# Last RMSNorm of a decoder trunk: second half's squares and factor in PSUM, one activation table for logarithm and exponential, two outputs on GpSimd

## The chip, the cores and the metric

The kernel runs on one NeuronCore of a Trainium2 chip. The metric is the device time of one execution in microseconds (us); the median over runs is compared. The engines are called by their names in the profile: PE is TensorE (PEld its weight loads), DVE is VectorE, ACT is ScalarE, POOL is GpSimd, and SP is SyncE, which here only issues DMAs.

## What is computed

A two-layer decoder trunk on a sequence of 1024 tokens of width 1024, in float32: each layer has a pre-norm mixer (the first a retention and an RWKV-7 group, the second sliding-window attention) and a SwiGLU FFN, both added to the residual `h`. At the end stands one more RMSNorm, which is what the change is about:

```python
def rms_norm(x, g):
    xf = x.astype(jnp.float32)
    y = xf * lax.rsqrt(jnp.mean(xf * xf, axis=-1, keepdims=True) + RMS_EPS)
    return (y * g.astype(jnp.float32)).astype(x.dtype)

def reference(x, ...):
    h = x
    for layer in range(DEPTH):          # DEPTH = 2
        n = rms_norm(h, norm1_g[layer])
        ...
        h = h + mix
        n = rms_norm(h, norm2_g[layer])
        h = h + swiglu(n, ffn_w_gate[layer], ffn_w_up[layer], ffn_w_down[layer])
    return rms_norm(h, final_g)
```

## The kernel before

The residual stands transposed in SBUF: features on the 128 partitions, in 8 tiles (`h(k)`, k = 0 to 7) of 512 tokens, for each of two halves of the sequence (`hf` 0 and 1). Matrix products split each float32 operand into a high and a low part (`split`, `vsplit`, `wsplit`) and do three matmuls for each product: ScalarE casts the high part (lines L356 and L1348), GpSimd or VectorE subtracts to get the low part (L358, L1349), and `prod` issues the three matmuls (L1175 to L1177).

The FFN's down projection (`down`) treats the two halves of the sequence and pairs of output columns together, with sums and differences of blocks (one level of a Strassen-like scheme), so that each product goes into more than one column's sum. Its helper `vop` holds every VectorE addition of it, so all of them have the line L1375: `u<-ps_m,u` and `y<-ps_r,u` gather products, `h<-h,u` and `h<-h,ps_f` add to the residual. In the last group of the last layer the columns of half 0 get their final values first. `down` then hands back control (`yield`), the last norm of half 0 is traced, and the rest of `down` follows: four products into the banks `f`, `f`, `f`, `y`, each of which is added to h(1), h(3), h(5), h(7) of half 1, and then four more on top of them in the same banks, which are added to h(0), h(2), h(4), h(6). The PSUM pool of this phase has three banks `f`, two `m`, and one each of `r`, `c` and `y`. The one bank `c` and the bank `r` last hold products of the phase before these eight.

`final_r` computes one half's factor. For each of the 8 columns, in the order in which they get ready, ScalarE squares `h(k)` into an SBUF tile `nq` (L1626) and multiplies `h(k)` in place by the norm's gain (L1627); VectorE adds the square to the running sum, in place in the square's tile (L1629). A matmul with a constant matrix of 1/1024 (L1632) sums over the partitions and gives every partition the mean: one for the sum of the first seven squares and one for the eighth. A float32 matmul shows as two records. ScalarE then takes the logarithm (L1634) and exp(-0.5 x) (L1635) into the tile `y`. When a function is not in the activation table set that ScalarE holds, a table load stands before it, with the same line. `final_out` multiplies `h(k)` by the factor (L1642) and stores it with a DMA on SP's queue (L1643): 256 KB each, all of half 0 on GpSimd and all of half 1 on VectorE.

The order in which each engine works its queue is settled when the program is built: a scheduler with a timing model takes the traced instructions as they become ready, and prefers those that were traced earlier. So squares of half 0 stand on ScalarE between the weight casts of the last products. `keep` pins an instruction behind the one that was traced before it on the same engine. Each engine works its queue in order.

Of the kernel before, what the change touches and what calls it, by code (L numbers as in the profile page):

```python
# [12 lines left out]
AF = mybir.ActivationFunctionType  # L13
ALU = mybir.AluOpType
AX = mybir.AxisListType

P = 128
T = 1024
HT = 512
# [185 lines left out]
class Kern:  # L205
# [1411 lines left out]
    def final_r(self, hf, pool, order, n):  # L1617


        nc = self.nc  # L1620
        h = self.kt(self.h[hf])
        ps = self.pst("m", [P, HT])
        acc = None
        for i, k in enumerate(order):
            sq = self.t(self.pp, [P, HT], "nq", 4)
            nc.scalar.activation(sq, h(k), AF.Square)  # L1626
            nc.scalar.activation(h(k), h(k), AF.Copy, scale=self.col("nf", k))  # L1627
            if 0 < i < n:
                nc.vector.tensor_tensor(out=sq, in0=acc, in1=sq, op=ALU.add)  # L1629
            acc = sq  # L1630
            if i >= n - 1:
                nc.tensor.matmul(ps, self.cst["ones"], sq, start=i == n - 1, stop=i == KT - 1)  # L1632
        r = self.t(pool, [P, HT], "y", 2)
        nc.scalar.activation(r, ps, AF.Ln, bias=self.cst["eps"][:, 0:1])  # L1634
        nc.scalar.activation(r, r, AF.Exp, scale=-0.5)  # L1635
        return r

    def final_out(self, hf, r, order, engines):
        nc = self.nc
        h = self.kt(self.h[hf])  # L1640
        for k, e in zip(order, engines):
            (nc.gpsimd if e == "p" else nc.vector).tensor_tensor(out=h(k), in0=h(k), in1=r, op=ALU.mult)  # L1642
            nc.sync.dma_start(self.out[k, :, hf * HT : (hf + 1) * HT], h(k))  # L1643


def trunk(tc, A, out):
    with ExitStack() as ctx:
        K = Kern(ctx, tc, A, out)
# [4 lines left out]
        def close(*gs):  # L1653
            for g in gs:
                g.__exit__(None, None, None)

        def run(f):
            for _ in f:
                pass
# [55 lines left out]
        r = K.factor_of(1, sp, "c")  # L1715
# [43 lines left out]
        r = K.factor_of(1, sp)  # L1759
# [17 lines left out]
        f = K.down(1, fp, fz, K.form_down(1, NP - 1, x, ts), X)  # L1777
        next(f)
        order = (0, 2, 4, 6, 1, 3, 5, 7), (1, 3, 5, 7, 0, 2, 4, 6)
        r0 = K.final_r(0, fz, order[0], 7)  # L1780
        run(f)
        r1 = K.final_r(1, fz, order[1], 7)
        K.final_out(0, r0, order[0], "pppppppp")
        K.final_out(1, r1, order[1], "vvvvvvvv")
        close(gp, gf, gz, K.ghx, g1, gy)


# [53 lines left out]
```

## Time and profile before

| | us |
|---|---|
| median of 3 runs | 2376.92 |
| lowest and highest run | 2371.43, 2380.17 |
| profiled execution | 2374.81 |
| its span in the profile | 2373.0 |
| mean granted TensorE clock | 0.99 |
| busy: PE, DVE, ACT, POOL | 2312.1, 1667.4, 1054.7, 948.4 |

The span is what the records of the profile cover; the execution's own time is 1.81 us longer. Busy times are sums of instruction durations. Times of single instructions below count from the span's start, so that 2340 lies 33 us before its end. "DVE nq L1629" is a VectorE instruction of line 1629 that writes a tile `nq`; "issue" in the chain is time in which nothing is waited for.

### The profile page before, as it was taken

What the parts mean: (1) busy time and instruction counts of PE and PEld (TensorE: products, weight loads), DVE (VectorE), ACT (ScalarE), POOL (GpSimd) and SP (SyncE); (2) the same over time, 40 slices, a digit from 0 to 9 for tenths busy, and PEclk for the clock granted to TensorE, in tenths of its full rate; (3) what the DMA queues carried; (4) which work ended last, traced back from release to release, by engine and by line L of the source; (5) the groups of instructions that cost most, each with busy time, mean ns of one, the idle gap of its engine ahead of it and who ended that gap; (6) DMA issues with size and microseconds to landing.
All of it is one profiled execution on the core that took longest, in us unless ns stands there. A gap on an engine that the chain in (4) does not pass through costs nothing. (4 is left out here: it accounts for less than half of the span.)

```text
span 2373.0 us, 35626 instructions
## 1 busy us (share of the span) xinstructions
PE 2312.1 (97%) x13092; PEld 1828.9 (77%) x13092; DVE 1667.4 (70%) x2630; ACT 1054.7 (44%) x1946; POOL 948.4 (40%) x746
## 2 busy tenths in 40 slices
PE   8999999999999999999999999999999999999997
PEld 6777777777777888888778877777787888877885
DVE  6876865774667358887675668567548778888776
ACT  5354533324456333333333556557645333333335
POOL 3123221201342057776667300002103577767665
PEclk9999999999999999999999999999999999999998
DMA  7555544443445545554554321232236465547652
GB/s 271 203 199 197 176 154 132 128 115 114 148 164 183 208 164 206 211 197 163 218 220 142 123 66 64 71 127 71 100 128 221 170 216 213 209 175 280 245 193 87
DMA packets 167741, 395.92 MB, mean 167 GB/s; under 512 B 42896, under 2 KB 45584, under 8 KB 167568
## 3 DMA queue, kind: packets, MB, share of 16 engines
q1 hardware_dynamic: 164448, 388.15, 47.8%
q10 hardware_dynamic: 2832, 4.45, 0.5%
q8 instruction: 104, 1.70, 0.3%
q0 software_dynamic: 288, 1.05, 0.1%
q14 instruction: 69, 0.57, 0.1%
HBM read 271.29 MB, written 116.92 MB: 164 GB/s over the span
## 5 line engine op out<-in xcount | busy, mean ns | idle before, releaser
L240 PE MATMUL ps_f<-n,w 128*128 128x512 f32 x1440 | 385.6, 415 | 8.6 <-ACT w L335 6.4
L240 PEld LDWEIGHTS ps_f<-n,w 128*128 128x128 f32 x1440 | 268.2, 192 | 93.6 <-issue 24.5
L335 ACT CAST w<-wr 128x512 fp32r<-128x512 f32 x244 | 147.9, 612 | 182.9 <-PE ps_f L352 73.1
L336 POOL TENSOR_TENSOR w<-wr,w 128x512 fp32r<-128x512 f32 x68 | 92.1, 1363 | 280.0 <-ACT w L335 223.0
L336 DVE TENSOR_TENSOR w<-wr,w 128x512 fp32r<-128x512 f32 (+1 forms) x176 | 123.8, 706 | 71.5 <-ACT w L335 71.3
L336 POOL TENSOR_TENSOR w<-wq,w 128x512 fp32r<-128x512 f32 x92 | 130.5, 1431 | 29.2 <-ACT w L335 27.2
L351 PE MATMUL ps_f<-n,w 128*128 128x512 f32 x356 | 141.7, 398 | 0.0
L352 PE MATMUL ps_f<-n,w 128*128 128x512 f32 x356 | 141.0, 396 | 0.6 <-POOL w L336 0.6
L350 PE MATMUL ps_f<-n,w 128*128 128x512 f32 x356 | 140.8, 396 | 0.6 <-ACT n L1601 0.5
L1182 DVE TENSOR_TENSOR nq<-ps_m,u 128x512 f32<-128x512 f32 x88 | 58.8, 685 | 104.3 <-PE ps_m L1177 104.2
L336 POOL TENSOR_TENSOR wx<-wr,wx 128x512 fp32r<-128x512 f32 x8 | 10.6, 1319 | 301.8 <-ACT wx L335 301.6
L1175 PE MATMUL ps_f<-n,w 128*128 128x512 f32 x298 | 118.5, 398 | 4.7 <-DVE h L1375 3.1
L1175 PE MATMUL ps_m<-n,w 128*128 128x512 f32 x300 | 117.5, 392 | 1.5 <-DVE h L1375 1.5
L1176 PE MATMUL ps_f<-n,w 128*128 128x512 f32 x298 | 117.2, 393 | 0.1
L1176 PE MATMUL ps_m<-n,w 128*128 128x512 f32 x300 | 116.8, 389 | 0.0
L1177 PE MATMUL ps_m<-n,w 128*128 128x512 f32 x300 | 116.8, 389 | 0.0
L1177 PE MATMUL ps_f<-n,w 128*128 128x512 f32 x298 | 116.7, 393 | 0.0
L358 POOL TENSOR_TENSOR n<-nq,n 128x512 fp32r<-128x512 f32 x54 | 91.5, 1707 | 8.9 <-ACT n L356 8.9
L1175 PE MATMUL ps_m<-cb,w 128*128 128x512 f32 x240 | 93.4, 389 | 1.0 <-DVE nq L1182 1.0
L1176 PE MATMUL ps_m<-cb,w 128*128 128x512 f32 x240 | 93.4, 389 | 0.0
L1177 PE MATMUL ps_m<-cb,w 128*128 128x512 f32 x240 | 93.4, 389 | 0.0
L1349 POOL TENSOR_TENSOR w<-wd,w 128x512 fp32r<-128x512 f32 (+1 forms) x53 | 76.0, 1444 | 34.8 <-ACT w L1348 34.8
(525 smaller groups left out, 6467.1 us busy)
## 6 DMA issues: line engine op xcount, KB each, us to landing
hc<-n SPq DMA_DIRECT2D x74, 512.0 KB, 2.6
wsp<-w SPq DMA_DIRECT2D x54, 512.0 KB, 3.3
w<-wsp SPq DMA_DIRECT2D x54, 512.0 KB, 3.4
wq<-in_w_gate SPq DMA_DIRECT2D x44, 512.0 KB, 4.3
u<-u SPq DMA_DIRECT2D x88, 256.0 KB, 2.9
n<-hc SPq DMA_DIRECT2D x43, 512.0 KB, 5.5
wr<-in_w_in SPq DMA_DIRECT2D x34, 512.0 KB, 4.8
hid<-n SPq DMA_DIRECT2D x66, 256.0 KB, 2.0
```

The lines of the kernel that those rows point to most:

```text
L240: self.nc.tensor.matmul(out, lhsT, rhs, **kw)
L335: nc.scalar.copy(hi[:, :n], raw[:, c])
L336: self.lo.tensor_tensor(out=lo[:, :n], in0=raw[:, c], in1=hi.bitcast(F32)[:, :n], op=ALU.subtract)
L350: nc.tensor.matmul(ps, hi, rh, start=k == 0, stop=False)
L351: nc.tensor.matmul(ps, hi, rl, start=False, stop=False)
L352: nc.tensor.matmul(ps, lo, rh, start=False, stop=k == n - 1)
L358: e.tensor_tensor(out=lo, in0=src, in1=hi.bitcast(F32), op=ALU.subtract)
L1175: mm(ps, hi, xh, start=first and k == 0, stop=False, skip_group_check=True)
L1176: mm(ps, hi, xl, start=False, stop=False, skip_group_check=True)
L1177: mm(ps, lo, xh, start=False, stop=last and k == len(w) - 1, skip_group_check=True)
L1182: add = lambda o, x, y: V.tensor_tensor(out=o, in0=x, in1=y, op=ALU.add)
L1349: nc.gpsimd.tensor_tensor(out=lo, in0=v, in1=hi.bitcast(F32), op=ALU.subtract)
```

## The change

In the second half, the squares that are added (all but the first and the last) are written to the PSUM bank `c`, and the running sum goes to an SBUF tile `nq` of its own. The second half's factor is written twice by two exponentials of the same logarithm: first into the PSUM bank `r`, for VectorE, which makes six outputs with it, and then into SBUF, for GpSimd, which makes the last two. An activation table set that holds logarithm and exponential is loaded ahead of both factors, pinned behind the last ScalarE instruction traced so far (a cast of the last products' inputs). The first half is otherwise as it was, with all its outputs on GpSimd.

```diff
@@ final_r(self, hf, pool, order, n)
         ps = self.pst("m", [P, HT])
         acc = None
         for i, k in enumerate(order):
-            sq = self.t(self.pp, [P, HT], "nq", 4)
+            if hf and 0 < i < n:
+                sq = self.pst("c", [P, HT])
+            else:
+                sq = self.t(self.pp, [P, HT], "nq", 4)
             nc.scalar.activation(sq, h(k), AF.Square)
             nc.scalar.activation(h(k), h(k), AF.Copy, scale=self.col("nf", k))
             if 0 < i < n:
-                nc.vector.tensor_tensor(out=sq, in0=acc, in1=sq, op=ALU.add)
+                o = self.t(self.pp, [P, HT], "nq", 4) if hf else sq
+                nc.vector.tensor_tensor(out=o, in0=acc, in1=sq, op=ALU.add)
+                sq = o
             acc = sq
             if i >= n - 1:
                 nc.tensor.matmul(ps, self.cst["ones"], sq, start=i == n - 1, stop=i == KT - 1)
         r = self.t(pool, [P, HT], "y", 2)
         nc.scalar.activation(r, ps, AF.Ln, bias=self.cst["eps"][:, 0:1])
+        if not hf:
+            nc.scalar.activation(r, r, AF.Exp, scale=-0.5)
+            return r, None
+        rp = self.pst("r", [P, HT])
+        nc.scalar.activation(rp, r, AF.Exp, scale=-0.5)
         nc.scalar.activation(r, r, AF.Exp, scale=-0.5)
-        return r
+        return r, rp
 
     def final_out(self, hf, r, order, engines):
         nc = self.nc
         h = self.kt(self.h[hf])
         for k, e in zip(order, engines):
-            (nc.gpsimd if e == "p" else nc.vector).tensor_tensor(out=h(k), in0=h(k), in1=r, op=ALU.mult)
+            if e == "p":
+                nc.gpsimd.tensor_tensor(out=h(k), in0=h(k), in1=r[0], op=ALU.mult)
+            else:
+                nc.vector.tensor_tensor(out=h(k), in0=h(k), in1=r[1], op=ALU.mult)
             nc.sync.dma_start(self.out[k, :, hf * HT : (hf + 1) * HT], h(k))
@@ trunk
         next(f)
         order = (0, 2, 4, 6, 1, 3, 5, 7), (1, 3, 5, 7, 0, 2, 4, 6)
+        K.keep(tc.nc.scalar.preload_act_table_set("natural_log_exp_and_others"))
         r0 = K.final_r(0, fz, order[0], 7)
         run(f)
         r1 = K.final_r(1, fz, order[1], 7)
         K.final_out(0, r0, order[0], "pppppppp")
-        K.final_out(1, r1, order[1], "vvvvvvvv")
+        K.final_out(1, r1, order[1], "vvvvvvpp")
```

## The prediction

> **What bounds the kernel now.** I read the head of the profile's page first, then the chain of work that ended last, in order of time, for the last 40 us, then the groups of instructions by line for the same stretch, and last the busy time in short windows. Times are microseconds from the span's start.
>
> ```profile
> span 2373.0 us, 35626 instructions
> PE 2312.1 (97%) x13092; PEld 1828.9 (77%) x13092; DVE 1667.4 (70%) x2630; ACT 1054.7 (44%) x1946; POOL 948.4 (40%) x746
> ```
>
> TensorE is busy 97% of the span, so no edit on another engine can move anything but the stretches in which TensorE has run out of work. The timeline has the last matmuls of two of the four column groups of the final GEMM, three groups apart:
>
> ```profile
> 2345.51 0.39 PE L1177 MATMUL ps_f<-n,w 128*128 128x512 f32 x1
> ...
> 2351.63 0.39 PE L1177 MATMUL ps_y<-n,wr 128*128 128x512 f32 x1
> ```
>
> So a group takes (2351.63 - 2345.51) / 3 = 2.04, its results are there at 2345.90, 2347.94, 2349.98 and 2352.02, and then 2373.0 - 2352.0 = 21 us are left in which only the last norm runs. Everything the change touches lies there or shortly before. The chain through it (start, duration, engine, written tile, line):
>
> ```profile
> 2340.98 1.08 DVE nq L1629
> 2342.05 0.61 DVE h L1375
> 2342.69 0.64 ACT nq L1626
> 2343.35 0.72 ACT h L1627
> 2344.09 1.28 ACT L1634
> 2345.39 0.69 ACT y L1634
> 2346.09 1.28 ACT L1635
> ...
> 2348.02 0.53 ACT nq L1626
> 2348.57 1.36 DVE nq L1629
> ...
> 2351.24 1.66 DVE nq L1629
> ...
> 2354.18 1.60 DVE nq L1629
> ...
> 2357.09 1.62 DVE nq L1629
> 2358.74 3.39 PE ps_m L1632 x4
> 2362.16 0.69 ACT y L1634
> 2362.86 1.28 ACT L1635
> 2364.15 0.65 ACTq L1836
> ...
> 2364.82 0.69 DVE h L1642
> ```
>
> The pieces without a tile at L1634 and L1635 are table loads, 1.28 each. Three of them are on the chain; the second half's logarithm has its load beside the matmul. The middle is one loop, four times over: add of a square (L1629), residual add of the next column (L1375), square of it (L1626), add. It runs 2.9 a turn although TensorE delivers a column every 2.04: the columns wait for the loop. Why the adds are slow is in the groups (busy us, mean ns | idle before):
>
> ```profile
> L1642 POOL TENSOR_TENSOR h<-h,y 128x512 f32<-128x512 f32 x8 | 11.7, 1504 | 6.6 <-ACT y L1635 6.6
> L1629 DVE TENSOR_TENSOR nq<-nq,nq 128x512 f32<-128x512 f32 x6 | 8.0, 1333 | 9.0 <-ACT nq L1626 9.0
> ...
> L1642 DVE TENSOR_TENSOR h<-h,y 128x512 f32<-128x512 f32 x8 | 4.9, 686 | 5.5 <-ACT y L1635 5.5
> ...
> L1375 DVE TENSOR_TENSOR h<-h,ps_f 128x512 f32<-128x512 f32 x4 | 2.7, 674 | 0.0
> ```
>
> With both inputs in SBUF and GpSimd busy, a VectorE add takes 1333 on average; with GpSimd idle the same shape takes 686 (L1642); with one input in PSUM 674, though GpSimd was multiplying beside most of them. GpSimd pays too:
>
> ```profile
> 2351.05 1.30 POOL L1642 TENSOR_TENSOR h<-h,y 128x512 f32<-128x512 f32 x1
> 2352.29 1.73 POOL L1642 TENSOR_TENSOR h<-h,y 128x512 f32<-128x512 f32 x1
> ```
>
> 1.30 with no SBUF-only VectorE add beside it, 1.73 with one.
>
> **The change part by part.** The sum is made against the profiled execution: 2374.81, a span of 2373.0 and 1.81 around it. That is 2.1 below the median of the runs shown, 2376.92.
>
> *Squares in PSUM.* Six adds (the second half's) get one PSUM input; I take 0.68 for each, by the L1375 row. The first, 1.08 at 2340.98, has a GpSimd subtraction beside it (L1349, last row of the next fence) and leads to the first half's logarithm: 0.40 less. Then 1.36, 1.66, 1.60 and 1.62 become 0.68: 0.68 + 0.98 + 0.92 + 0.94 = 3.52. (The second of the six does not wait for GpSimd and gains nothing.) No row has ScalarE writing PSUM; the nearest are its reads:
>
> ```profile
> 2297.25 0.59 ACT L1410 COPY u<-ps_f 128x512 f32<-128x512 f32 x1 [1.04 <-PE ps_f L1177]
> ...
> 2334.82 0.68 DVE L1375 TENSOR_TENSOR u<-ps_c,u 128x512 f32<-128x512 f32 x1
> ...
> 2340.49 1.02 POOL L1349 TENSOR_TENSOR wr<-ws,wr 128x384 fp32r<-128x384 f32 x1 [2.09 <-ACT wr L1348]
> ```
>
> From 0.59 to the logarithm's 0.69, so a square, now 0.64, changes by -0.05 to +0.05; over five squares and the exponential on the path that is -0.3 to +0.3. I take 0, since the operation stays the same. [...]
>
> The new wait: the one bank "c" makes the next square wait for the add before it. Behind a square in ScalarE's queue stand the scale copy (L1627) and the logarithm; VectorE's next add waits for all that. It costs nothing: the next square already waits for L1375, which VectorE runs after that add. If that order changed, the cover would go, and the price is the one add, 0.68. The bank's last reader in the GEMM is a VectorE operation that ended by 2335.5 (2334.82 and 0.68), before the first such square.
>
> *One table, loaded ahead.* Loads at 2344.09 and 2346.09 vanish, 2 x 1.28 = 2.56 off the chain, since ScalarE is the last to be ready there (the square at 2348.02 starts behind the exponential). The load at 2362.86 vanishes: 1.28. The new load stands on ScalarE behind the last cast traced before it:
>
> ```profile
> 2318.89 0.62 ACT L356 CAST n<-hr 128x512 fp32r<-128x512 f32 x1
> 2319.71 0.63 ACT L1626 ACTIVATE nq<-h 128x512 f32<-128x512 f32 x1 [0.20 <-DVE h L1375]
> 2320.24 0.50 ACT L1348 CAST w<-wd 128x384 fp32r<-128x384 f32 x1
> ...
> 2321.75 2.89 POOL L1349 TENSOR_TENSOR w<-wd,w 128x384 fp32r<-128x384 f32 x2
> ...
> ACT w L1348 <- PE ps_r L1177: 1.8, 2, 1.5
> ```
>
> It takes 2319.5 to 2320.8, so the square and the weight cast move by about 1.1. Cover: the GpSimd half of that cast's split does not start before 2321.75 in this trace, and casts of this stretch wait up to 1.5 for TensorE to free a buffer (last row). 0, at worst 1.28. [...] The chain has 0.02 between the scale copy's end (2344.07), the load, and the logarithm (2345.39), so I count the load alone.
>
> *What is late next.* Take 0.40 + 2.56 and the add savings off the four residual adds and they want to start at 2346.30, 2348.27, 2350.25 and 2352.22, against TensorE's 2345.90, 2347.94, 2349.98 and 2352.02: the loop only just stays behind the GEMM. TensorE is the floor; at most 0.2 more can come out of this loop.
>
> *The ones-matmuls* (L1632), unchanged in code, change in speed:
>
> ```profile
> 2341.68 1.02 PE L1632 MATMUL ps_m<-nq,c_ones 128*128 128x512 f32 x2
> ...
> 2354.00:2355.00 1.00, 0.00 (x0) 0.00 (x0) 0.81 (x1) 0.87 (x2) 1.00 (x2) 0.88 0.11 43
> 2355.00:2356.00 1.00, 0.00 (x0) 0.00 (x0) 1.00 (x2) 0.00 (x0) 1.00 (x2) 0.50 0.57 219
> ```
>
> A pair took 1.02 for the first half; for the second, after 6.7 of idle TensorE and at a granted clock of 0.50 (the figure after POOL's), two pairs took 3.39. After the change TensorE idles 0.2 before the first pair and 0.5 before the second, so the clock stays. From the last add's end: residual add 0.61, square 0.66, weight load 0.2, pair 1.02, together 2.5 where it was 3.46 (2358.70 to 2362.16): 0.9 less (0 if the clock fell).
>
> *Six outputs on VectorE, two on GpSimd.* The factor is written twice; the copy for GpSimd comes one exponential (0.65) later. VectorE would end after 6 x 0.61 + 0.1 = 3.8 instead of 4.9, GpSimd after 0.65 + 2 x 1.30 = 3.3 if its eight products of half 0 are done: they start about 3.0 earlier, at 2345.1, and at 1.3 each end at 2355.5, before the factor at 2356.1. The two stores stand last on SP, so nothing waits behind them. But the stores are the limit:
>
> ```profile
> 2366.00:2371.60 5.60, 0.00 (x0) 0.00 (x0) 3.73 (x7) 0.00 (x0) 0.00 (x0) 0.50 0.97 374
> ...
> 2367.00:2368.00 1.00, 0.00 (x0) 0.00 (x0) 1.00 (x3) 0.00 (x0) 0.00 (x0) 0.50 1.07 412
> ```
>
> The DMA share is 0.97 over the 5.6 us in which the eight outputs leave, at about 410 GB/s when full: 8 x 256 KB at that rate is 5.1, more than either multiply time. First output to end stays as it is, 8.2 after the exponential. I count 0 (at best 1.1).
>
> *Sum:* 0.40 + 2.56 + 3.52 + 0.9 + 1.28 = 8.7. Span 2364.3, execution 2366.1; from the median, 2376.92 - 8.7 = 2368.2.
>
> **The rivals.**
>
> *The loads stay* (the table set isn't kept up to the logarithm, and the old pairs are loaded again). For it: nothing in this trace shows the combined set. Then the adds alone save 0.40 + 3.52 = 3.9, and the last add ends at 2354.8, where the clock is already falling (0.88), so the matmul gains nothing sure: 2373.0. Against it: squares and copies ran after both sets here without a load between.
>
> *The end shrinks as well*: if the stores are paced by the producers and not by the 16 DMA engines, the last product 1.1 earlier counts: 9.8, 2367.1. Against: the share above 1 for whole microseconds.
>
> *A stall around each load* that goes with it. From rows it can be only the 0.02 gaps on both sides of three loads, 0.1 more: 2368.1. [...]
>
> *Slower: ScalarE's queue order.* If the new load changes the order so that the weight casts (L1348) of the last GEMM each stand behind a square and its scale copy (0.64 + 0.72), TensorE stalls for its weights. Ten such casts follow 2319.5; 10 x 1.36 = 13.6, less 8.7, is 4.9 slower: 2381.8. It decides from 0.9 of stall per cast. For it: casts and squares share one in-order queue. Against: one load can cost only 1.28 once, and the casts have up to 1.5 of slack.
>
> **How the numbers follow.** Forecast 0.74, loads stay 0.12, shorter end 0.09, slower 0.04, stall 0.01. About 0.5% (11.9 us) is what a measurement of this kernel can tell from no change. The forecast and three of the rivals lie within it, and the runs of before spread 4.4 to either side: a tenth of forecast and shorter end, with the stall, gives 0.10 for faster, and I round up to 0.12; the slower rival gives 0.04; 0.84 is left. The range takes in 3.9 of gain at the upper end and 9.8 at the lower with 4 of spread below and 2 above: 2363 to 2375.
>
> **What would show it.** Right: no load at the lines of the logarithm and exponential, one near 2319; adds of the second half near 0.68 with GpSimd busy; residual adds starting at most 0.4 behind 2345.9, 2347.9, 2350.0, 2352.0; GpSimd products near 1.3; ones-matmul pair near 1.0; the DMA share still near 1 for 5 us and 8.2 from exponential to end. Wrong: loads still there, squares into PSUM well over 0.69, waits of TensorE for L1348 after 2320, or a tail below 7.5.

## The result, and the profile after

| | before | after |
|---|---|---|
| median of 8 runs, us | 2376.51 | 2366.32 |
| lowest and highest | 2371.43, 2380.17 | 2360.48, 2371.24 |
| profiled execution's span | 2373.0 | 2364.8 |
| last GEMM matmul of TensorE ends | 2352.02 | 2352.64 |
| from there to the end of the span | 20.98 | 12.16 |

The ratio of the times is 0.9956 (95% interval 0.9943 to 0.997): 10.5 us less, between 7.1 and 13.5. That is 0.44%. The interval does not reach a ratio of 1, but the gain stays a little below the half per cent that the prediction takes as what a measurement of this kernel can tell. The forecast was 8.7 less. The two profiled executions differ by 0.6 already when TensorE ends its last product, so what the change does is read from there on: 8.8 of 21.0 are gone. Below, "tail" is this stretch, from the end of the last matmul of line L1177 to the end of the span.

First the head of the page after; TensorE's busy time is the same within 2 us:

```profile
span 2364.8 us, 35624 instructions
PE 2313.9 (98%) x13092; PEld 1829.7 (77%) x13092; DVE 1664.2 (70%) x2628; ACT 1051.8 (44%) x1944; POOL 952.2 (40%) x748
```

The chain that ended last, after. L1629 is now the square, L1633 the add, L1630 the scale copy, L1637 the ones-matmul, L1639 the logarithm, L1641 and L1644 the exponentials:

```profile
2341.56 0.69 DVE nq L1633
2342.25 0.61 DVE h L1375
...
2343.52 0.73 ACT h L1630
2344.24 0.58 ACT y L1639
2344.85 0.63 ACT y L1641
2345.48 0.50 ACT ps_c L1629
2346.00 0.69 DVE nq L1633
2346.69 0.61 DVE h L1375
...
2347.95 0.69 DVE nq L1633
...
2349.95 0.69 DVE nq L1633
...
2352.00 0.69 DVE nq L1633
2352.69 0.69 DVE h L1375
2353.40 0.64 ACT nq L1629
...
2354.08 1.14 PE ps_m L1637 x2
2355.25 0.70 ACT y L1639
2355.97 0.61 ACT ps_r L1644
```

No table load stands on it any more, all adds take 0.69, and a turn of the loop lasts 1.95 to 2.05 instead of 2.67 to 2.94. The groups of the tail (mean ns after the bar) have GpSimd's products at 1295 instead of 1504 and the squares into PSUM at 597:

```profile
L1653 POOL TENSOR_TENSOR h<-h,y 128x512 f32<-128x512 f32 x10 | 12.5, 1295 | 5.2 <-ACT y L1641 3.4 <-ACT y L1645 1.7
...
L1633 DVE TENSOR_TENSOR nq<-nq,ps_c 128x512 f32<-128x512 f32 x6 | 4.1, 689 | 5.7 <-ACT ps_c L1629 5.7
L1655 DVE TENSOR_TENSOR h<-h,ps_r 128x512 f32<-128x512 f32 x6 | 3.7, 681 | 3.2 <-ACT ps_r L1644 3.2
L1629 ACT ACTIVATE ps_c<-h 128x512 f32<-128x512 f32 x6 | 3.6, 597 | 2.5 <-DVE h L1375 2.5
```

The timeline shows the one load that is left, and TensorE's last product with the residual add that takes it:

```profile
2320.21 1.28 ACT L1793 ACT_TABLE_LOAD   x1
...
2352.25 0.39 PE L1177 MATMUL ps_y<-n,wr 128*128 128x512 f32 x1
...
2352.68 0.69 DVE L1375 TENSOR_TENSOR h<-h,ps_y 128x512 f32<-128x512 f32 x1
```

The product is complete at 2352.64 and its residual add starts at 2352.68. Before, that add started at 2358.61, 6.6 behind TensorE; now the loop has caught up with it.

### The profile page after: what moved, and what is told of

The parts are those of the page before. It is cut to its first block, busy times and chain, and to the rows that moved or that the text cites. A ratio compares the mean times of both kernels' runs of the same rounds, so it can differ in the third digit from the quotient of the medians.

```text
span 2364.8 us, 35624 instructions
## 1 busy us (share of the span) xinstructions
PE 2313.9 (98%) x13092; PEld 1829.7 (77%) x13092; DVE 1664.2 (70%) x2628; ACT 1051.8 (44%) x1944; POOL 952.2 (40%) x748
## 3 DMA queue, kind: packets, MB, share of 16 engines
q0 software_dynamic: 288, 1.05, 0.1%
## 5 line engine op out<-in xcount | busy, mean ns | idle before, releaser
L1177 PE MATMUL ps_m<-n,w 128*128 128x512 f32 x300 | 116.9, 390 | 0.0
L1177 PE MATMUL ps_f<-n,w 128*128 128x512 f32 x298 | 116.7, 393 | 0.0
L1177 PE MATMUL ps_m<-cb,w 128*128 128x512 f32 x240 | 93.4, 389 | 0.0
```

The costliest lines, as they stand in the source:

```text
L1177: mm(ps, lo, xh, start=False, stop=last and k == len(w) - 1, skip_group_check=True)
```

## The experiments

All twelve profiles (before, after and ten experiments) are read with the same three marks; runs without a ratio are one profile each. "Factor" is the end of the first exponential of the second half, from which the products can start.

| run | GEMM to factor | factor to end | tail | ratio to before |
|---|---|---|---|---|
| before | 12.78 | 8.20 | 20.98 | |
| the change | 3.94 | 8.22 | 12.16 | 0.9956 (0.9943 to 0.997) |
| e1, table only | 9.26 | 8.26 | 17.52 | 0.9993 (0.9981 to 1.0005) |
| e2, squares only | 8.58 | 8.19 | 16.77 | 0.9987 (0.9975 to 0.9999) |
| e3, split only | 13.14 | 8.21 | 21.35 | 0.9997 (0.9986 to 1.0008) |
| e4, no split | 3.96 | 8.24 | 12.20 | 0.996 (0.9947 to 0.9974) |
| e5, half stores | 3.94 | 7.22 | 11.16 | |
| e6, two banks | 4.00 | 8.19 | 12.19 | |
| e7, first output in halves | 3.93 | 8.23 | 12.16 | |
| e8, two queues | 3.93 | 8.23 | 12.16 | |
| e9, table, no GpSimd products | 4.35 | 8.19 | 12.54 | |
| e10, table, TensorE kept at work | 8.15 | 8.18 | 16.33 | |

### The parts alone: e1 to e4

Theory: loads and contended adds give the gain, the split gives nothing because the stores' bytes set the end. Rivals: loads hidden, or dearer by a stall; the parts work only together; producers set the end.

e1 adds only the load to the kernel before:

```diff
+        K.keep(tc.nc.scalar.preload_act_table_set("natural_log_exp_and_others"))
         r0 = K.final_r(0, fz, order[0], 7)
```

> Only the combined table loaded ahead; squares in SBUF, one factor in SBUF, all outputs of the second half on VectorE. Measure: the tail, from the end of TensorE's last GEMM matmul (L1177) to the end of the span; 20.98 before, 12.16 after the whole change. Theory (three loads of 1.28 come off the path, nothing else; adds stay near 1.6 beside GpSimd, TensorE idles about 4 us and its ones-matmuls stay at 3.4): tail 17.1, 3.8 less, time about 2372.7. [...] Rival, the loads were hidden and the adds alone made the gain: 21.0.

In the chain of e1:

```profile
2358.80 1.62 DVE nq L1629
2360.46 3.80 PE ps_m L1632 x4
2364.28 0.69 ACT y L1634
2365.00 0.64 ACT y L1635
```

The tail is 3.5 shorter where 3.8 was expected. 0.4 of the expectation went into the ones-matmul, which took 3.80, against 3.39 before. So the loads made 3.46 + 0.41 = 3.87, and three times 1.28 is 3.84: the run shows no stall beside them.

e2 adds only the hunk that puts the second half's squares into PSUM:

```diff
-            sq = self.t(self.pp, [P, HT], "nq", 4)
+            if hf and 0 < i < n:
+                sq = self.pst("c", [P, HT])
+            else:
+                sq = self.t(self.pp, [P, HT], "nq", 4)
...
+                o = self.t(self.pp, [P, HT], "nq", 4) if hf else sq
```

> Only the squares of the second half in PSUM, with a sum tile of their own; four table loads as before, one factor in SBUF, all outputs of the second half on VectorE. Theory (contention with GpSimd leaves five adds of the path, 0.40 + 3.52): adds near 0.69, GpSimd products near 1.3, tail 17.1; if the clock has not yet fallen when the ones-matmuls come (TensorE idle 2.8 us) up to 0.9 less, 16.2. Rival, the two edits only work together, since the loop is held by the late first-half factor: adds at 0.69 but tail above 19. Time about 2372 to 2373.

The tail is 4.2 shorter, between the two values expected; adds at 0.69, GpSimd's eight products in 9.9 instead of 11.7. So each edit works alone. But 3.5 and 4.2 make 7.7, and both together (e4) take off 8.8: 1.1 comes only when both are there. It lies in the stretch from the last add's end to the logarithm's start: 3.46 before, 3.86 in e1, 3.33 in e2 and 2.56 in the change. In e2 the two pairs of ones-matmuls took 3.09 (in the change 1.13 and 1.12), and the logarithm's table load, which is still there, ended last: at 2359.96, 0.17 behind them. e10 shows what makes the stretch long in e1.

e3 has only the two exponentials and "vvvvvvpp", e4 everything but these (its last lines are those of before).

> Only the factor written twice (PSUM and SBUF), six outputs of the second half on VectorE and two on GpSimd; squares in SBUF and four table loads as before. Theory (the stores' bytes set the end): last product about 1.1 earlier, yet from the end of the first exponential to the end of the span 8.2 as before, tail 21.0, time as before. Rival, producers set the end: 7.1 and tail 19.9.

> The whole change without the split: squares in PSUM, table loaded ahead, one factor in SBUF, all eight outputs of the second half on VectorE. Theory (the stores' bytes set the end): tail 12.2 and 8.2 from exponential to end, like the whole change, time about 2366.3. Rival, producers set the end: tail 13.3.

In the chain of e3 the six products on VectorE end at 2368.1, 3.7 after the factor, where eight took 4.9; the end of the span, 2372.6, stays 8.21 behind the factor:

```profile
2363.78 0.61 ACT ps_r L1639
2364.42 0.69 DVE h L1650
2365.10 0.60 DVEq L1844
2365.70 2.39 DVE h L1650 x4
```

e4 has a tail of 12.20 and the same time as the whole change. The split, alone or with the rest, moves nothing. (e3's tail is 0.4 longer than that of before: its ones-matmul took 3.80, as in e1.)

### Why the end does not move: e5, e8, e7

e5 stores only half of each output of the second half, e8 issues every other store from ScalarE's queue:

```diff
 # e5
-            nc.sync.dma_start(self.out[k, :, hf * HT : (hf + 1) * HT], h(k))
+            w = HT // 2 if hf else HT
+            nc.sync.dma_start(self.out[k, :, hf * HT : hf * HT + w], h(k)[:, :w])
 # e8
-            nc.sync.dma_start(self.out[k, :, hf * HT : (hf + 1) * HT], h(k))
+            (nc.scalar if hf and j % 2 else nc.sync).dma_start(...)
```

> The whole change, but of each output of the second half only the first 256 of 512 columns are stored (128 KB instead of 256 KB); the products are all made. Measure: from the end of the first exponential of the second half's factor to the end of the span, 8.2 before and after the change. Theory (the stores' bytes set the end): the stream of stores takes about 2.6 instead of 5.1, the last product at 3.7 becomes the limit, and the stretch comes to 6.4 to 7.0. Rival, producers and a fixed latency set the end: 8.2 stays.

> The whole change, with every other store of the second half issued from ScalarE's queue instead of SP's. Theory (the 16 DMA engines are full, share near 1, about 410 GB/s): 8.2 from exponential to end stays. Rival, the one queue limits the stores: faster than 410 GB/s, and 7.1 or less.

Windows of the two (PEclk, DMA share and GB/s are the last three figures), e5 first:

```profile
2359.00:2360.00 1.00, 0.00 (x0) 0.00 (x0) 0.87 (x2) 0.00 (x0) 0.40 (x1) 0.69 0.76 265
2360.00:2361.00 1.00, 0.00 (x0) 0.00 (x0) 0.00 (x0) 0.00 (x0) 0.00 (x0) 0.50 0.74 260
```

```profile
2354.00:2355.00 1.00, 0.00 (x0) 0.00 (x0) 1.00 (x3) 0.00 (x0) 1.00 (x2) 1.00 1.04 401
2355.00:2356.00 1.00, 0.00 (x0) 0.00 (x0) 0.87 (x2) 0.00 (x0) 0.40 (x1) 0.69 1.04 399
```

With half the bytes the DMA engines are no longer full (0.76) and the end comes 1.0 earlier, although the products are all made at the same times: the stores set the end. But 7.2 is above the 6.4 to 7.0 expected. VectorE's last product of e5 ends at 2359.87, and two more microseconds of stores follow, at 260 and 248 GB/s instead of about 405. At that rate a store of 128 KB takes about 0.5, not the 0.32 of the expectation, so by these rows the stores were the limit here too, and not the last product. Each row of a store also went from 2 KB to 1 KB; whether that made the rate fall, no run shows. With two queues (e8) the engines are as full as with one (share 1.04 to 1.06 in both), and nothing moves: SP's queue is not the bound. The stores moved at 399 to 410 GB/s for four microseconds in e8, at 404 to 408 in the change.

e7 then tries to use that, by letting the stores begin earlier:

```diff
+                if k == order[0]:
+                    for o in (0, HT // 2):
+                        c = slice(o, o + HT // 2)
+                        nc.vector.tensor_tensor(out=h(k)[:, c], in0=h(k)[:, c], in1=r[1][:, c], op=ALU.mult)
+                        nc.sync.dma_start(self.out[k, :, hf * HT + o : hf * HT + o + HT // 2], h(k)[:, c])
+                    continue
```

> The whole change, with the first output of the second half multiplied and stored in two halves of 256 columns, so that the stores begin about 0.28 earlier. Theory (the stores' bytes set the end): from exponential to end 7.9 instead of 8.2, tail 11.9. Rival, the end hangs on the last product, which comes 0.13 later for the extra instruction: 8.3 to 8.4.

A miss: 8.23. The windows of e7 from 0.9 after the factor on:

```profile
2354.00:2355.00 1.00, 0.00 (x0) 0.00 (x0) 1.00 (x3) 0.00 (x0) 1.00 (x1) 1.00 0.47 165
2355.00:2356.00 1.00, 0.00 (x0) 0.00 (x0) 1.00 (x3) 0.00 (x0) 1.00 (x2) 0.99 0.92 345
2356.00:2357.00 1.00, 0.00 (x0) 0.00 (x0) 0.83 (x2) 0.00 (x0) 0.29 (x1) 0.50 1.06 408
```

The stores did begin earlier (0.47 in the first of these windows, against 0.36 in the change at the same distance from the factor), but then there was a gap (0.92 against 1.05 in the second): the second output ends 1.38 after the factor, 0.06 later than in the change, for the extra instruction. So "the stores' bytes set the end" is only half of it: VectorE makes an output every 0.60 and the DMA engines take 0.64 for it (256 KB at about 408 GB/s), and an earlier start is worth nothing unless the second output comes earlier as well. That reading is argued from these rows, not tried.

### The new wait: e6

```diff
-                sq = self.pst("c", [P, HT])
+                sq = self.pst("cr"[i % 2], [P, HT])
```

> The whole change, with the squares in the two PSUM banks c and r by turns, so that a square need not wait for the add of the one before it. Theory (that wait is covered by the wait for the residual add): tail from the end of TensorE's last GEMM matmul to the end of the span 12.2 as with one bank. Rival, the one bank holds the loop: residual adds start earlier against TensorE's columns and the tail is up to 0.7 shorter, 11.5.

12.19: the wait for the one bank is covered. A turn of the loop that TensorE does not hold up lasts 1.95 with two banks (adds at 2348.76, 2350.71 and 2352.67) and 1.95 with one (2346.00 and 2347.95 in the chain after).

### What slows the adds: e9

e1 with the first half's eight products left out:

```diff
-            (nc.gpsimd if e == "p" else nc.vector).tensor_tensor(out=h(k), in0=h(k), in1=r, op=ALU.mult)
+            if hf:
+                nc.vector.tensor_tensor(out=h(k), in0=h(k), in1=r, op=ALU.mult)
```

> The table loaded ahead, squares in SBUF, one factor in SBUF, all outputs of the second half on VectorE, and the first half's eight products with the factor left out (its columns are stored unmultiplied), so that GpSimd is idle beside the loop. Theory (GpSimd is what slows the adds, the PSUM operand only gets out of its way): adds of the loop near 0.69 with both inputs in SBUF, residual adds right behind TensorE's columns, tail from the end of TensorE's last GEMM matmul to the end of the span 12.2, as with the whole change, against 17.5 for the table alone. Rival, an add with both inputs in SBUF is slow in this loop for another reason: adds at 1.6, tail 17.5.

```profile
2354.49 0.69 DVE L1629 TENSOR_TENSOR nq<-nq,nq 128x512 f32<-128x512 f32 x1 [0.70 <-ACT nq L1626]
2355.09 0.68 DVE L1375 TENSOR_TENSOR h<-h,ps_f 128x512 f32<-128x512 f32 x1
```

An add with both inputs in SBUF takes 0.69 in the same loop once GpSimd is idle: it is GpSimd that costs the 0.9, and PSUM is a way around it. The profile before shows how the two meet. The add of 2351.24 began while the GpSimd product of 2351.05 ran; that product ended at 2352.35 and the add at 2352.89, 0.54 later. Each of the five slow adds ended 0.54 to 0.55 after the GpSimd instruction that was running when it began, as if it had waited for that instruction's end. The GpSimd products that began while an add was under way took 1.72 to 1.75, the others 1.27 to 1.30. So the prediction read one row wrongly: the product of 1.30 did have an SBUF-only add beside it, but had begun first. And its mean of 1333 for adds with GpSimd busy has in it one add of 0.69 (at 2343.35) beside which GpSimd was idle. The tail is 12.54; the 0.3 above 12.2 comes from the first add, which still ran beside GpSimd's last weight subtraction (1.08), so that the loop stayed 0.4 behind TensorE.

### What the parts give only together: e10

e1 with two ones-matmuls more, of the running sum, whose results nobody reads:

```diff
+            if hf and i == 5:
+                for tag in "rc":
+                    nc.tensor.matmul(self.pst(tag, [P, HT]), self.cst["ones"], acc, start=True, stop=True)
```

> The table alone, as in the run of that name, with two more ones-matmuls whose results nobody reads: they take the running sum after the sixth square into the banks r and c, so that TensorE works in the wait before the two real ones (the last sum gets a tile of its own). Theory (the clock falls because TensorE idles about 4 us there): the granted clock stays near 1, from the last add's end to the logarithm's start 2.6 instead of 3.9, tail 16.2 instead of 17.5. Rival, those matmuls are slow for another reason: 3.9 and 17.5 or more.

Chain of e10, then a window of e10 and one of e1, each at the start of the real ones-matmuls (the granted clock is the third figure from the right):

```profile
2352.66 1.62 DVE nq L1630
2354.28 0.61 DVE h L1375
...
2355.59 1.14 PE ps_m L1637 x2
2356.76 0.70 ACT y L1639
```

```profile
2354.00:2355.00 1.00, 0.67 (x2) 0.30 (x2) 0.88 (x2) 0.09 (x1) 1.00 (x1) 1.00 0.44 168
```

```profile
2360.00:2361.00 1.00, 0.54 (x1) 0.50 (x2) 1.00 (x2) 0.00 (x0) 1.00 (x1) 0.50 0.43 166
```

From the last add's end to the logarithm 2.48 instead of 3.86, tail 16.33, where e1 had 17.52: work added to TensorE makes the tail shorter, and the clock stays at 1.00 until the logarithm has begun. In the change itself the two savings bring the ones-matmuls so close to the GEMM (the first pair starts 0.10 behind it) that no such filler is needed: the clock is 1.00 there until 2359. Against the kernel before, this stretch is 0.90 shorter in the change, 0.13 shorter in e2 and 0.40 longer in e1. The difference, 0.90 - 0.13 + 0.40 = 1.17, is the 1.1 that the parts alone did not give.

## Why the prediction was right

Term by term on the chains before and after, with the end of TensorE's last product as the common zero:

| step | forecast | measured |
|---|---|---|
| first add beside GpSimd (1.08 to 0.69), up to the first logarithm | 0.40 | 0.47 |
| first half's two loads, up to the next add | 2.56 | 2.72 |
| four adds | 3.52 | 3.48 |
| the loop's three turns without their adds (3.90 to 3.93) | 0 | -0.03 |
| last add to logarithm (3.46 to 2.56) | 0.9 | 0.90 |
| second half's load (2.64 to 1.33, logarithm and exponential) | 1.28 | 1.31 |
| split of the outputs (8.20 to 8.22) | 0 | -0.02 |
| sum | 8.7 | 8.8 |

- **Bound.** The tail behind TensorE's last product is all that moved; from 2352.64 on the measured sum is 8.8. The forecast span was 2364.3; the profile has 2364.8, of which 0.6 had come in before the tail.
- **Squares in PSUM.** The size was right and so was the reason (e9). Writing PSUM, which no earlier row showed, costs ScalarE 0.60 for a square, less than the 0.63 into SBUF, inside the -0.05 to +0.05 that the prediction allowed. A source in PSUM did not make VectorE slower: 689 and 681 with one (L1633 and L1655 after), 686 without (L1642 before).
- **Table.** One load at 2320.2, as forecast about 2319.5, and its cover held: TensorE has no wait behind it that was not there before. A stall at each load, which the prediction gives 0.01 and counts toward faster, no run shows: in e1 taking the three loads off the path made 3.87, and their own durations are 3.84. The rival of loads that stay fell with the profile.
- **TensorE as the next bound.** The loop was to stay 0.3 behind TensorE; its residual adds start 0.04 to 0.09 behind and so it has met the floor. The first add and the first half's loads gave 0.23 more than forecast. The floor took back about 0.15: the last two turns lasted 2.00 and 2.05 where a free one lasts 1.95. The rest of the turns, the shorter squares above all, gave about 0.12 of that back. That the sum came out within 0.2 is in part luck: such small errors cancelled.
- **Ones-matmuls.** 0.9 forecast, 0.90 measured, and the clock goes with it: in e10, at 1.00, this stretch took 2.48 where e1 took 3.86 at 0.50. The pair took 1.14 where the sum had 1.02.
- **Split.** Nothing, as forecast. The reason given, that the stores set the end, holds for the change as it stands (e3, e4, e5), but it was put too simply: half the bytes did not take half the time (e5), and producers and stores are matched within a few hundredths (e7).
- **The slower rival**, casts held up on ScalarE, had no sign: TensorE's one wait for L1348 is 0.2, as before.

What is left open: the ratio of the times says 10.5 less and the tail says 8.8. The interval holds both, and nothing ahead of the tail has been found that would make the difference. e4, which has the same tail as the change, gives 9.5 less (6.2 to 12.6) against 33 runs of the kernel before, made with e1 to e4.

## What to carry to other kernels

When one engine is busy 97% of the span, read the stretch behind its last instruction as a kernel of its own, and cost each step there by its row and by what is late next. Where VectorE has to add two SBUF tiles while GpSimd works, let the engine that makes one of them write it to a free PSUM bank: here the adds then took 0.69 and GpSimd's products 1.30. Before splitting the last products between engines, see whether the DMA engines behind them are already full (here a share of 1.04 to 1.06 for four microseconds).

## What had not been expected of the hardware

The granted clock falls to half (0.50) for a few microseconds in the middle of the kernel too, and not alike in each execution, although the work is the same up to the last norm. The traces of the kernel before, the change, e1 and e4 all have such stretches, of about 3.4 or 6.8 us each (0.96 or 0.91 over 40 us; before, the clock is 0.50 from 289.7 to 296.5). The windows 280 to 320 and 440 to 480 have one in each of the four; others, like the two shown here, have one in some. Two 40 us windows of e1, then of e4:

```profile
1200.00:1240.00 40.00, 35.83 (x146) 29.07 (x145) 29.47 (x32) 12.47 (x21) 25.61 (x17) 0.91 0.55 202
1480.00:1520.00 40.00, 35.77 (x184) 24.42 (x183) 25.07 (x62) 22.22 (x57) 0.00 (x0) 0.91 0.12 41
```

```profile
1200.00:1240.00 40.00, 37.76 (x166) 30.67 (x165) 30.53 (x33) 13.38 (x24) 27.84 (x19) 1.00 0.60 226
1480.00:1520.00 40.00, 35.77 (x191) 25.90 (x190) 24.48 (x56) 22.87 (x56) 0.00 (x0) 1.00 0.16 53
```

0.91 over 40 us is about 7 us at half clock. TensorE's last product ended at 2356.38 in e1 and at 2347.80 in e4, a spread as large as the change's whole gain. The clock makes only a part of it. Up to that product e1 had 30.7 us at half clock and e4 23.9, so at most half of those 6.8 us, an estimated 3.4 of the 8.6, was lost to it. TensorE's busy time up to there was 2308.7 and 2305.8, so 5.7 of the 8.6 us are time in which it had no work. Over those 33 runs of the kernel before, the five with a mean clock of 0.988 or less took 2380.1 on average and the ten with 0.991 or more 2373.6. So clock and time go together, but no run set the clock, and what is cause and what is effect stays open. This spread is why parts worth 3 to 4 us could be told in the tail of a profile and hardly in the times.
